# The last feed-forward block's left half by seven products, among the third column block

## The chip, the cores and the metric

The kernel runs on one core of one Trainium2 chip. The metric is the time of one execution on the device in microseconds (us); the time of the kernel before is the median of three runs, 1326.16 us (1325.57 to 1326.43). About 0.2% is what a measurement of this kernel can tell from no change.

## What is computed

One decoder block on 256 tokens of width 2048, all in fp32:

```python
merged = jax.nn.sigmoid(ga) * y_a + jax.nn.sigmoid(gb) * y_b
mix = jnp.einsum('bsd,de->bse', merged, w_out)
h = layer_norm(ALPHA * x + mix, ln1_gain, ln1_bias)
a = jnp.square(jax.nn.relu(jnp.einsum('bsd,df->bsf', h, w_ff1) + b_ff1))
y = layer_norm(ALPHA * h + jnp.einsum('bsf,fd->bsd', a, w_ff2) + b_ff2, ln2_gain, ln2_bias)
```

`w_ff1` is 2048 x 8192 and `w_ff2` 8192 x 2048. `y_a` and `y_b` come from attention and from a gated branch; the change doesn't touch them.

## The kernel before

**Numbers.** Every large product is made of three matmuls in the type fp32r: both operands are split into a high and a low part, and high x high, high x low and low x high are added in PSUM. Activations are split once (`hilo`, L92). Weights are split as they come: a chunk of 512 rows x 512 columns (1 MB) is loaded by SP into one of three `raw` buffers, and used as two pieces of 2 x 128 rows. For each piece ACT writes the high part (L188) and DVE the low part (L157, `emit_low`). When the low part of a chunk's second piece is out, SP's load of the chunk three further on is issued.

**Order.** The program is one list of steps, written by hand; a step is the matmuls of one piece. Each engine works through its own instructions in the order in which they are emitted. `emit_splits` emits splits as far ahead as there are split buffers: the six of RING, so five steps ahead, each taken over when PE has finished the step that used it. Pieces of the last block's column blocks may also use the buffers in LATE. `at(s, f)` emits `f` behind step `s`: that is how evictions' follow-ups, joinings and statistics get their place on DVE.

**Feed-forward.** The 8192 inner columns are worked in eight blocks of 1024. The first layer of a block (steps F) makes `a`; the second layer adds the block's share to `y`, which holds both token tiles (128 tokens each) x 2048. The second layer's columns come in four column blocks of 512. By the plain way (steps E) a column block takes 48 matmuls of 512 columns: 2 token tiles x 8 pieces of 128 rows x 3.

**Seven products.** In the blocks of `SUMMED` (1 to 6 of 0 to 7) column blocks 0 and 1 are made by `products` instead, a Strassen-Winograd scheme: the 2 x 2 arrangement of token tiles and column blocks, and of row halves, takes seven products of 12 matmuls (P1 to P7, 84 in place of 96). It needs sums of activations (`sum_of_acts`, four DVE additions and two splits for each of four pieces) and sums of weights. The sums of weights are made by DMA: POOL loads a block of `w_ff2` into the buffer `held` (L623) and adds other blocks to it with accumulating transfers (L625, L632). There are two such buffers. Buffer 0 holds, one after the other, what P1, P5, P6 and P4 need; the next addition is issued when DVE has written the second low part of the product before:

```python
("P1", plain(0, 0), 0, held_add(u, 0, 1), 0),
("P5", summed(0), 0, held_add(u, 1, 1), 1),
("P6", summed(1), 0, held_add(u, 1, 0), 2),
```

P7 uses buffer 1; P2 and P3 use plain chunks through SP. A product gathers in one of two PSUM buffers named `aux`, in turn, so a product needs the eviction of the last but one. DVE evicts it (L664) into `acc` or `y`. At the end eight joinings (`collect`, L694) add what lies in `acc` to `y`; the sums in `acc` run over all blocks, so these joinings are made once.

**Mixed blocks.** `mixed(b)` interleaves the first layer of block b with the products and steps E of block b - 1, by the list `ORDER` (L36). In it, three steps F stand between P5 and P6.

**The last block and the end.** In the kernel before block 7 takes the plain way: column block 0 for both token tiles, then 1, 2 and 3 for token tile 0, then for token tile 1 (its column block 3 in two halves of 256). The eight joinings lie behind the first steps of it. Statistics (`bn_stats`, 256 columns each) follow each eviction. `ln2_stats` and four `ln2_block`s finish token tile 0 under the matmuls of token tile 1; `ln2_last` (L767) finishes token tile 1 behind the last eviction, with three filling matmuls and one pair of small ones on PE.

**The output projection** is made the same way: P1, P5 and P6 lie among the last groups of the projections before it.

## Time and profile before

| | |
|---|---|
| median of the runs | 1326.16 us |
| profiled execution, its own time | 1326.2 us |
| its span in the profile | 1324.5 us |
| PE busy | 1312.9 us, 99% |
| DVE busy | 939.0 us, 71% |
| ACT busy | 691.0 us, 52% |
| granted TensorE clock, mean | 0.998 |

PE is TensorE, DVE is VectorE, ACT is ScalarE, POOL is GpSimd and SP the engine that issues most loads. Busy time tells which engine is full over the whole span, but matmuls are pipelined and overlap, so a busy PE is not yet PE at its peak. The views by stretch and in order of time tell which wait ends last in one place. In them an instruction has its start, its duration, and in brackets how long its engine stood idle before it and which instruction released it. The 1.7 us between span and time lie outside the profiled program.

### The profile page before, as it was taken

What the parts mean: (1) busy time and instruction counts of PE and PEld (TensorE: products, weight loads), DVE (VectorE), ACT (ScalarE), POOL (GpSimd) and SP (SyncE); (2) the same over time, 40 slices, a digit from 0 to 9 for tenths busy, and PEclk for the clock granted to TensorE, in tenths of its full rate; (3) what the DMA queues carried; (4) which work ended last, traced back from release to release, by engine and by line L of the source; (5) the groups of instructions that cost most, each with busy time, mean ns of one, the idle gap of its engine ahead of it and who ended that gap; (6) DMA issues with size and microseconds to landing.
All of it is one profiled execution on the core that took longest, in us unless ns stands there. A gap on an engine that the chain in (4) does not pass through costs nothing. (4 is left out here: it accounts for less than half of the span.)

```text
span 1324.5 us, 17423 instructions
## 1 busy us (share of the span) xinstructions
PE 1312.9 (99%) x6832; PEld 1111.0 (84%) x6832; DVE 939.0 (71%) x1426; ACT 691.0 (52%) x938; POOL 51.7 (4%) x57
## 2 busy tenths in 40 slices
PE   9999999999999999999999999999999999999998
PEld 6888888888888888889888888888888888888886
DVE  6554678565545689788769768678677796786776
ACT  4444465454544556545545366455555564555641
POOL 0000000000000001000000100010000000100000
PEclk9999999999999999999999999999999999999999
DMA  9866545546555569772874988987887879978561
GB/s 321 289 195 206 176 137 182 191 160 222 191 191 190 187 169 291 244 230 71 283 255 148 284 219 289 248 242 247 217 280 229 237 242 251 252 224 236 178 254 64
DMA packets 140003, 288.83 MB, mean 218 GB/s; under 512 B 5256, under 2 KB 7824, under 8 KB 139024
## 3 DMA queue, kind: packets, MB, share of 16 engines
q1 hardware_dynamic: 120592, 240.26, 53.5%
q0 software_dynamic: 19184, 47.20, 16.8%
q8 instruction: 53, 0.87, 0.3%
q10 hardware_dynamic: 144, 0.26, 0.1%
q14 instruction: 30, 0.25, 0.1%
HBM read 285.59 MB, written 2.11 MB: 217 GB/s over the span
## 5 line engine op out<-in xcount | busy, mean ns | idle before, releaser
L157 DVE TENSOR_TENSOR w<-raw,w 128x1024 fp32r<-128x1024 f32 (+1 forms) x438 | 529.2, 1218 | 300.8 <-ACT w L188 299.7
L188 ACT ACTIVATE w<-raw 128x1024 fp32r<-128x1024 f32 (+1 forms) x438 | 456.7, 1053 | 411.8 <-PE mm L254 289.7
L252 PE MATMUL mm<-hT,w 128*128 128x512 f32 x960 | 339.4, 394 | 0.8 <-DVE sum L277 0.8
L252 PE MATMUL mm<-xs,w 128*128 128x512 f32 x896 | 315.7, 395 | 0.0
L254 PE MATMUL mm<-hT,w 128*128 128x256 f32 x1024 | 276.0, 279 | 0.0
L254 PE MATMUL mm<-xs,w 128*128 128x256 f32 x896 | 250.0, 279 | 0.0
L252 PEld LDWEIGHTS mm<-hT,w 128*128 128x128 f32 x960 | 180.0, 187 | 44.3 <-DVE sum L277 1.1
L252 PEld LDWEIGHTS mm<-xs,w 128*128 128x128 f32 x896 | 167.9, 187 | 39.5
L254 PEld LDWEIGHTS mm<-hT,w 128*128 128x128 f32 x1024 | 188.0, 188 | 2.7
L254 PEld LDWEIGHTS mm<-xs,w 128*128 128x128 f32 x896 | 168.0, 187 | 0.2
L242 PE MATMUL mm<-w,a 128*128 128x512 f32 (+1 forms) x328 | 128.1, 390 | 0.0
L241 PE MATMUL mm<-w,a 128*128 128x512 f32 (+1 forms) x328 | 128.0, 390 | 0.0
L240 PE MATMUL mm<-w,a 128*128 128x512 f32 (+1 forms) x328 | 127.8, 390 | 0.0
L157 DVE TENSOR_TENSOR w<-held,w 128x1024 fp32r<-128x1024 f32 x70 | 85.6, 1223 | 39.3 <-ACT w L188 38.9
L188 ACT ACTIVATE w<-held 128x1024 fp32r<-128x1024 f32 x70 | 73.9, 1058 | 64.7 <-PE mm L242 26.6
L240 PEld LDWEIGHTS mm<-w,a 128*128 128x128 f32 x328 | 61.8, 188 | 14.3
L242 PEld LDWEIGHTS mm<-w,a 128*128 128x128 f32 x328 | 61.7, 188 | 14.0
L241 PEld LDWEIGHTS mm<-w,a 128*128 128x128 f32 x328 | 61.8, 188 | 13.9
L240 PE MATMUL mm<-w,xs 128*128 128x512 f32 x120 | 49.4, 412 | 0.3 <-ACT w L188 0.3
L241 PE MATMUL mm<-w,xs 128*128 128x512 f32 x120 | 47.7, 397 | 1.3 <-DVE w L157 1.3
L277 DVE TENSOR_TENSOR sum<-mm,half 128x256 f32<-128x256 f32 x136 | 48.9, 418 | 0.0
L242 PE MATMUL mm<-w,xs 128*128 128x512 f32 x120 | 47.6, 397 | 0.0
(193 smaller groups left out, 1512.8 us busy)
## 6 DMA issues: line engine op xcount, KB each, us to landing
raw<-in_w_ff_dram SPq DMA_DIRECT2D x116, 1024.0 KB, 6.5
raw<-in_w_in_dram SPq DMA_DIRECT2D x68, 1024.0 KB, 5.1
held<-in_w_ff_dram POOLq DMA_DIRECT2D x36, 1024.0 KB, 8.5
raw<-in_w_out_dram SPq DMA_DIRECT2D x14, 1024.0 KB, 5.4
raw<-in_w_pa_dram SPq DMA_DIRECT2D x8, 1024.0 KB, 5.1
raw<-in_w_pb_dram SPq DMA_DIRECT2D x8, 1024.0 KB, 5.1
held<-in_w_out_dram POOLq DMA_DIRECT2D x6, 1024.0 KB, 8.5
raw<-in_w_in_dram SPq DMA_DIRECT2D x6, 512.0 KB, 7.2
```

The costliest lines, as they stand in the source:

```text
L157: nc.vector.tensor_tensor(h["lo"], sl, f32(h["hi"]), op=ALU.subtract)
L188: nc.scalar.activation(h["hi"], source(h), AF.Copy)
L240: nc.tensor.matmul(p, ah, hi[:, kk, cs], start=first and kk == 0, stop=False)
L241: nc.tensor.matmul(p, ah, lo[:, kk, cs], start=False, stop=False)
L242: nc.tensor.matmul(p, al, hi[:, kk, cs], start=False, stop=last and kk == n - 1)
L252: nc.tensor.matmul(p, hi[:, kk, ws_], av, start=st, stop=False)
L254: nc.tensor.matmul(p[:, :S], lo[:, kk, ws_], av[:, :S], start=False, stop=en)
L277: nc.vector.tensor_tensor(s, p[:, :S], t, op=ALU.add)
```

## The change

Block 7's column blocks 0 and 1 are made by the seven products too (`SUMMED` to 7). Its steps come in a new order, here with h0 and h1 for the two pieces of the second chunk of column block 2:

- column block 2's first chunk (two steps), P1, P3, P2, h0, P5, P7, h1, P6
- column block 3 for token tile 0 (four steps), P4, and column block 3 for token tile 1 in two halves.

The joinings come as soon as their sums are complete: the first behind P1, two behind P5, the others behind P6. Statistics of column blocks 0 and 1 are made by a new function `stats2` behind them. Token tile 0's norm blocks lie behind column block 3's first pass and among P4 and the last halves. The two wide rows of the last norm go to the buffers A4 and A5, since S6 and S13 now hold sums of activations; LATE shrinks to two buffers. In the output projection P5 and P6 come one group later, and the sums of activations are spread over twice as many steps.

```diff
@@ -605,7 +605,7 @@
         return ev
 
     NB = FF // 1024
-    SUMMED = range(1, NB - 1)
+    SUMMED = range(1, NB)
 
 
 
@@ -721,25 +721,30 @@
                     q[:0] = [(h, c == 0 and h == hs[0], c == g.nk // KC - 1 and h == hs[-1]) for h in hs]
             h, f, l = q.pop(0)
             add_step(h, "all", f, l)
-    LATE = ("A4", "A5", "W", "S5", "S10", "S11")
+    LATE = ("W", "S5")
 
     def ev_ff2(blk, c):
         def ev(i, p):
             t, half = i if isinstance(i, tuple) else (i, None)
             y = tiles["y", t][:, c * CW:(c + 1) * CW]
-            if blk == NB - 1 and c == 0:
-                tiles["st2", t] = small.tile([P, 8, 6], F32, name="st2")
+            if blk == NB - 1 and c == 2 and half is None and t == 0:
+                for k in range(NT):
+                    tiles["st2", k] = small.tile([P, 8, 6], F32, name="st2")
             if half is None:
                 nc.vector.tensor_tensor(y, y, p, op=ALU.add)
             else:
                 ys = y[:, half * S:(half + 1) * S]
                 nc.vector.tensor_tensor(ys, ys, p[:, half * S:(half + 1) * S], op=ALU.add)
             if blk == NB - 1:
-                for e in range(2) if half is None else (half,):
-                    nc.vector.bn_stats(tiles["st2", t][:, 2 * c + e, :], y[:, e * S:(e + 1) * S])
+                stats2(t, c, range(2) if half is None else (half,))
                 if c == 3 and half in (None, 1):
                     (ln2_last if t == NT - 1 else ln2_stats)(t)
         return ev
+
+    def stats2(t, c, parts=range(2)):
+        for e in parts:
+            nc.vector.bn_stats(tiles["st2", t][:, 2 * c + e, :],
+                               tiles["y", t][:, c * CW + e * S:c * CW + (e + 1) * S])
 
     def ln2_stats(t):
         mv = small.tile([P, 2], F32, name="mv", bufs=4)
@@ -845,14 +850,14 @@
     for i in range(4):
         add_group(Group(w_pa, i * CW, 8, quad("attnT"), "ws", ev_ya(i)))
         if i >= 2:
-            add_product(("P1", "P6")[i - 2])
+            add_product(("P1", "P5")[i - 2])
         if i == 2:
             for k in range(4):
-                at(len(steps) - 1 + k, lambda k=k: sum_of_acts(("S6", "W"), k, tiles["G", 1][:, 0, k, :]))
+                at(len(steps) - 1 + 2 * k, lambda k=k: sum_of_acts(("S6", "W"), k, tiles["G", 1][:, 0, k, :]))
         add_group(Group(w_pb, i * CW, 8, quad("gmlpT"), "ws", ev_yb(i), after=start_residual if i == 3 else None))
-        if i == 2:
-            at(len(steps), held_load, uo, 1)
-            add_product("P5")
+        if i == 3:
+            at(len(steps) - 3, held_load, uo, 1)
+            add_product("P6")
 
     g = Group(w_out, 2 * CW, 16, quad("merged"), "as", ev_out(2))
     for c, name in enumerate(("P7", "P4", "P3", "P2")):
@@ -913,19 +918,47 @@
                 load_post[j + 2 * i] = [lambda a=a: load_wide(*a)]
         for c in range(4):
             add_group(ff2(b - 1, c))
-    at(len(steps), free.extend, LATE[:4])
-    for i, a in enumerate((("ln2_b", ln2_b, "S6"), ("ln2_g", ln2_g, "S13"))):
+
+
+    at(len(steps), free.extend, LATE)
+    for i, a in enumerate((("ln2_b", ln2_b, "A4"), ("ln2_g", ln2_g, "A5"))):
         load_post[len(chunks) + i] = [lambda a=a: load_wide(*a)]
-    for i in range(8):
-        at(len(steps) + i // 2, collect, ff_unit(0), i)
-    add_group(ff2(NB - 1, 0))
-    hss = [add_pieces(ff2(NB - 1, c)) for c in range(1, 4)]
-    for part, hs in ((0, hss[0]), (0, hss[1]), (0, hss[2]), (1, hss[0]), (1, hss[1]), ((1, 0), hss[2]), ((1, 1), hss[2])):
+    u = ff_unit(NB - 1)
+    prods = products(u)
+    g2, g3 = ff2(NB - 1, 2), ff2(NB - 1, 3)
+
+    def columns2(c):
+        for n, h in enumerate(add_pieces(g2, None, (c,))):
+            add_step(h, "all", c == 0 and n == 0, c == 1 and n == 1)
+
+    def then(*fs):
+        for k, f in enumerate(fs):
+            at(len(steps) + k // 2, *f)
+
+    columns2(0)
+    add_product("P1")
+    then((collect, u, 0))
+    add_product("P3")
+    add_product("P2")
+    hs = add_pieces(g2, None, (1,))
+    add_step(hs[0], "all")
+    add_product("P5")
+    then((collect, u, 1), (collect, u, 6))
+    add_product("P7")
+    add_step(hs[1], "all", False, True)
+    add_product("P6")
+    then(*((collect, u, i) for i in (2, 3)), (stats2, 0, 0), (stats2, 0, 1), *((collect, u, i) for i in (4, 5, 7)),
+         (stats2, 1, 1))
+    hs = add_pieces(g3)
+    for h in hs:
+        s = add_step(h, 0, h == hs[0], h == hs[-1])
+    add_product("P4")
+    then((stats2, 1, 0))
+    for c in range(4):
+        at(s + 1 + c, ln2_block, 0, c)
+    for part in ((1, 0), (1, 1)):
         for h in hs:
-            s = add_step(h, part, h == hs[0], h == hs[-1])
-        if part == 0 and hs is hss[2]:
-            for c in range(4):
-                at(s + 1 + 2 * c, ln2_block, 0, c)
+            add_step(h, part, h == hs[0], h == hs[-1])
 
 
     xr = xT.rearrange("(k p) s -> p k s", p=P)
```

Where instructions stand now, at three places.

DVE's queue, behind the matmuls of the last mixed block. L157 writes a low part (`held` is the buffer of summed weights, `raw` a loaded chunk), L664 evicts a product, L733 or L734 evicts a column block, L694 is a joining. Before:

```order
L664 TENSOR_TENSOR y<-y,aux 128x512
L157 TENSOR_TENSOR w_10710<-raw,w_10710 128x1024
L157 TENSOR_TENSOR w_10725<-raw,w_10725 128x1024
L157 TENSOR_TENSOR w_10742<-raw,w_10742 128x1024
L733 TENSOR_TENSOR y<-y,mm 128x512 x2
L157 TENSOR_TENSOR w_10759<-raw,w_10759 128x1024
L157 TENSOR_TENSOR w_10764<-raw,w_10764 128x1024
```

Now, from P5's first low part to P6's second (P5: w_10845 and w_10855, P7: w_10867 and w_10877, P6: w_10887 and w_10897):

```order
L157 TENSOR_TENSOR w_10845<-held,w_10845 128x1024
L664 TENSOR_TENSOR acc<-acc,aux 128x512
L157 TENSOR_TENSOR w_10855<-held,w_10855 128x1024
L694 TENSOR_TENSOR y<-y,acc 128x512
L157 TENSOR_TENSOR w_10867<-held,w_10867 128x1024
L664 TENSOR_TENSOR y<-y,aux 128x512
L157 TENSOR_TENSOR w_10877<-held,w_10877 128x1024
L157 TENSOR_TENSOR w_10887<-held,w_10887 128x1024
L664 TENSOR_TENSOR y<-y,aux 128x512
L157 TENSOR_TENSOR w_10897<-held,w_10897 128x1024
```

All low parts of the last block read loaded chunks before; now six of these read the buffer of summed weights, and the eviction of P2 (the last L664) stands behind P6's first low part.

POOL's queue at its end, as a difference (L632 is an addition to buffer 0, L623 a plain load, L625 the addition to buffer 1):

```order
 L623 DMA held<-in_w_ff_dram 128x4x512
 L632 DMA held<-in_w_ff_dram 128x4x512 x3
-L1024 UNCONDITIONAL_BRANCH
-L1024 ISA
+L623 DMA held<-in_w_ff_dram 128x4x512
+L625 DMA held<-in_w_ff_dram 128x4x512
+L623 DMA held<-in_w_ff_dram 128x4x512
+L632 DMA held<-in_w_ff_dram 128x4x512 x3
```

Two loads and four additions have come behind what was the end of the queue.

DVE's queue ahead of `ln2_last`, from token tile 0's first norm block (L752 and L760, now L757 and L765) to the last statistics. Before:

```order
L752 SCALAR_TENSOR_TENSOR y<-y,mv,wide 128x512
L760 SCALAR_TENSOR_TENSOR y<-y,ry,wide 128x512
L752 SCALAR_TENSOR_TENSOR y<-y,mv,wide 128x512
L760 SCALAR_TENSOR_TENSOR y<-y,ry,wide 128x512
L733 TENSOR_TENSOR y<-y,mm 128x512
L739 BN_STATS st_10847<-y 128x6 x2
```

Now, with the joining and the statistics that precede it:

```order
L694 TENSOR_TENSOR y<-y,acc 128x512
L746 BN_STATS st_10971<-y 128x6 x2
L757 SCALAR_TENSOR_TENSOR y<-y,mv,wide 128x512
L765 SCALAR_TENSOR_TENSOR y<-y,ry,wide 128x512
L664 TENSOR_TENSOR y<-y,aux 128x512
L757 SCALAR_TENSOR_TENSOR y<-y,mv,wide 128x512
L765 SCALAR_TENSOR_TENSOR y<-y,ry,wide 128x512
L746 BN_STATS st_10971<-y 128x6 x2
```

In place of two column blocks of token tile 1, P4's eviction and the statistics of what it completes now stand among the norm blocks, two more of which follow before the last two evictions.

## Rows read from the trace of the kernel before

**Rows 1.** The page: the span, and busy time of each engine.

```profile
span 1324.5 us, 17423 instructions
...
PE 1312.9 (99%) x6832; PEld 1111.0 (84%) x6832; DVE 939.0 (71%) x1426; ACT 691.0 (52%) x938; POOL 51.7 (4%) x57
```

**Rows 2.** Busy time by stretch: length, then PE, PEld, DVE, ACT, POOL, clock, DMA share, GB/s.

```profile
1260.00:1280.00 20.00, 20.00 (x87) 16.20 (x87) 12.70 (x13) 8.59 (x9) 0.00 (x0) 1.00 1.03 392
1280.00:1313.00 33.00, 33.00 (x168) 27.91 (x167) 27.69 (x54) 3.46 (x4) 0.00 (x0) 1.00 0.10 37
```

**Rows 3.** PE in order of time (start, duration): first and last matmul of block 7.

```profile
1268.50 0.40 PE L240 MATMUL mm<-w,a 128*128 128x512 f32 x1
...
1312.82 0.28 PE L242 MATMUL mm<-w,a 128*128 128x256 f32 x1
```

**Rows 4.** DVE in order of time: the last eviction.

```profile
1313.14 0.42 DVE L736 TENSOR_TENSOR y<-y,mm 128x256 f32<-128x256 f32 x1 [1.95 <-PE mm L242]
```

**Rows 5.** By stretch, `aux` alone: P5 and P6 of the output projection (no POOL column).

```profile
498.97:502.57 3.60, 3.07 (x12) 2.07 (x12) 0.00 (x0) 0.00 (x0) 1.00 1.09 283
513.77:516.57 2.80, 2.80 (x12) 2.08 (x12) 0.00 (x0) 0.00 (x0) 1.00 1.12 198
```

**Rows 6.** Waits of PE from 470 to 1260, longest first: total, times, longest.

```profile
PE mm L252 <- DVE sum L277: 0.8, 1, 0.8
```

**Rows 7.** ACT in order of time: P1's first split in the last two mixed blocks.

```profile
1092.05 1.06 ACT L188 ACTIVATE w<-held 128x1024 fp32r<-128x1024 f32 x1 [1.33 <-PE mm L242]
...
1178.97 1.06 ACT L188 ACTIVATE w<-held 128x1024 fp32r<-128x1024 f32 x1 [1.24 <-PE mm L242]
```

**Rows 8.** DVE in order of time, 1173 to 1180, one block before the end.

```profile
1173.62 3.49 DVE L157 TENSOR_TENSOR w<-raw,w 128x1024 fp32r<-128x1024 f32 x3
1177.03 0.69 DVE L664 TENSOR_TENSOR y<-y,aux 128x512 f32<-128x512 f32 x1
1177.63 2.35 DVE L157 TENSOR_TENSOR w<-raw,w 128x1024 fp32r<-128x1024 f32 x2
```

**Rows 9.** DVE and POOL in order of time: P1's second low part, the addition behind it.

```profile
1182.87 1.22 DVE L157 TENSOR_TENSOR w<-held,w 128x1024 fp32r<-128x1024 f32 x1 [0.39 <-ACT w L188]
1184.47 1.27 POOL L632 DMA_DIRECT2D held<-in_w_ff_dram  x1 [20.67 <-DVE w L157]
```

**Rows 10.** Additions issued at 1010.63, 1184.47, 802.16, 749.05: last column, us to landing.

```profile
held<-in_w_ff_dram POOLq DMA_DIRECT2D x1, 1024.0 KB, 8.4
...
held<-in_w_ff_dram POOLq DMA_DIRECT2D x1, 1024.0 KB, 9.4
...
held<-in_w_ff_dram POOLq DMA_DIRECT2D x1, 1024.0 KB, 13.3
...
held<-in_w_ff_dram POOLq DMA_DIRECT2D x1, 1024.0 KB, 18.0
```

**Rows 11.** DVE in order of time, 1282 to 1305: joinings, an eviction, norm blocks.

```profile
1282.36 0.69 DVE L694 TENSOR_TENSOR acc<-acc 128x512 f32<-128x512 f32 x1
1283.09 0.69 DVE L694 TENSOR_TENSOR y<-y,acc 128x512 f32<-128x512 f32 x1
...
1296.41 0.69 DVE L733 TENSOR_TENSOR y<-y,mm 128x512 f32<-128x512 f32 x1 [1.05 <-PE mm L242]
...
1299.93 0.75 DVE L752 SCALAR_TENSOR_TENSOR y<-y,mv,wide 128x512 f32<-128x512 f32 x1
...
1302.83 0.68 DVE L733 TENSOR_TENSOR y<-y,mm 128x512 f32<-128x512 f32 x1
...
1304.21 0.74 DVE L752 SCALAR_TENSOR_TENSOR y<-y,mv,wide 128x512 f32<-128x512 f32 x1
```

**Rows 12.** By stretch, near the end of the span (the columns of Rows 2).

```profile
1318.00:1319.00 1.00, 0.49 (x1) 0.30 (x2) 0.94 (x2) 0.43 (x2) 0.00 (x0) 1.00 0.00 0
...
1320.00:1321.00 1.00, 0.00 (x0) 0.00 (x0) 0.27 (x1) 0.49 (x1) 0.00 (x0) 0.50 1.03 385
```

**Rows 13.** PE in order of time: the pair of small matmuls in `ln2_last`.

```profile
1318.51 1.35 PE L787 MATMUL aux<-y,dg 128*128 128x512 f32 x2 [1.98 <-ACT dg L783]
```

## The prediction

> **What bounds the kernel now.** I read the page's first part, then the last 55 us. PE is busy for 99% of the span, DVE for 71% [rows 1]. By stretch, PE has no gap from 1260 to 1313, DVE works 40.4 of these 53 us, and the DMA engines are full until 1280 (share 1.03) and nearly idle afterwards (0.10) [rows 2]. The last block's first matmul starts at 1268.50, its last at 1312.82 [rows 3]. DVE keeps up with PE there: for the last eviction it waited 1.95 us [rows 4]. From that eviction, at 1313.14, to the end of the span at 1324.5 are 11.36 us, which I call the ending; the change leaves it as it is. What counts is which engine brings the last eviction, and when.
>
> **The part that should gain.** Columns 0 and 1 of the last block take 96 matmuls now, seven products take 84. Twelve matmuls of 512 columns take PE 2.80 us, 0.233 each [rows 5]: the whole gain on PE there, and the length of a step of 12; one of 6 takes 1.40. Counted from 1268.50, PE without a wait would start P1 at 1274.1, P3 at 1276.9, P2 at 1279.7, h0 at 1282.5, P5 at 1285.3, P7 at 1288.1, h1 at 1290.9, P6 at 1293.7, column 3 of token tile 0 at 1296.5, P4 at 1302.1 and the two last halves at 1304.9 and 1307.7, ending at 1310.5. (h0 and h1 are the two halves of the third column block's second chunk.) In the middle of the program, P5 of the output projection took 3.60 us where P6 took 2.80 [rows 5]; the change gives its sums more time, and the order of POOL's queue there still leaves PE its cover, so I book a gain of 0.8 us, with 0 as the other end.
>
> **The chain of additions.** P5, P6 and P4 read one buffer, to which POOL adds another block of weights after each split. So each waits for: the last split of the product before, the addition, its own split. In the mixed blocks three steps of the first layer, 8.4 us, lie between P5 and P6, too; here only P7 and h1 do, 5.6 us. I follow the chain with durations from rows.
>
> 1. ACT splits the same product in two successive blocks at 1092.05 and 1178.97 [rows 7], so one block is 86.92 us. The block before the last now has the sums of activations, as the one before it had, so I move that one's DVE rows by 86.92. There, three low parts ran 1173.62 to 1177.11, an eviction began at 1177.03 and two more low parts ran 1177.63 to 1179.98 [rows 8]. Those two are now P1's: they end at 1266.9.
> 2. POOL issues 0.38 us after such an end (1182.87 + 1.22 to 1184.47) [rows 9]: at 1267.3.
> 3. Additions landed 8.4 to 9.4 us after their issue in ordinary stretches, and after 13.3 or 18.0 where transfers crowded [rows 10]. The stretch from 1260 to 1280 is crowded now [rows 2]; in the changed program a weight chunk and both rows of the last layer norm are queued there too. I take 11.5, about half way between 9.4 and 13.3: landed at 1278.8. The ends are 8.4 and 18.0.
> 4. ACT's high part takes 1.06 [rows 7], so DVE starts P5's first low part at 1280.0. Low parts follow each other by 1.14 and an eviction costs 0.60 before the next instruction [rows 8]: P5's second low part ends at 1280.0 + 1.14 + 0.60 + 1.22 = 1282.96. The addition for P6 is issued at 1283.3 and, in quieter DMA, lands 8.5 later at 1291.8; P6's first low part starts on DVE at 1293.05.
> 5. DVE had come to that instruction at 1286.5 (a joining 0.65, two low parts, an eviction). It waits 6.5 us with everything else behind it, P2's eviction included, which stands behind it in DVE's queue. P7 needs P2's PSUM buffer, since the products share two: it starts at 1293.05 + 1.14 + 0.68 = 1294.9 instead of 1288.1. **PE stands for 6.8 us.**
> 6. P6's second low part ends at 1296.0, the addition for P4 goes out at 1296.4 and lands at 1304.9; P4's first low part starts at 1306.05. DVE has only 7.2 us of other work in between and loses another 3 us.
>
> **DVE from there.** P4's two low parts, 2.3; two evictions with their statistics, 1.38 each (1302.83 to 1304.21) [rows 11], 2.76. Then P6's eviction and two dependent joinings, 0.73 each until the last (1282.36 to 1283.09) [rows 11], 2.06; four statistics, 1.34; two joinings, 1.33; the eviction of column 3, its statistics and the reciprocal root, 3.52 (1296.41 to 1299.93); a joining and statistics, 1.39; four norm blocks of 1.45 (two between 1299.93 and 1302.83), 5.8 [rows 11]; P4's eviction and statistics, 1.27. That is 2.3 + 2.76 + 16.7 = 21.8: DVE reaches the first of the two last evictions at 1327.8, some 15 us after PE has finished it, and the last one 0.85 later, at 1328.7. With the ending of 11.36 the span is 1340.0.
>
> Two corrections. PE idles for over 10 us before the last small matmuls. After it had stood from 1316.5, but for 1.35 us of work, its granted clock read 0.50 at 1320, the 1.2 GHz level, against 1.00, the 2.4 GHz level, at 1318 [rows 12]. Those two matmuls took 1.35 us [rows 13]; at half the clock they would cost up to 1.35 more; I take 0.7. The output projection gives 0.8 back. Span 1339.9. The profiled execution took 1326.2 for a span of 1324.5, so 1.7 us lie around it, and its time equals the median of the three runs (1326.16). **Forecast: 1341.6 us**, slower by 1.2%.
>
> **Edits at no cost.** The wide rows go to other buffers, free long before; fewer weight chunks are loaded. ACT has 3.46 us of work in the last 33 [rows 2], so its extra splits are covered until it too waits for the additions. The sums of activations in the block before are covered by PE there, as in the blocks before: from 470 to 1260 PE's longest wait is 0.8 us [rows 6].
>
> **Ends of the forecast itself.** All three additions in 8.4 us and no clock loss: 1338.7 - 0.8 + 1.7 = 1339.6. First addition 13.3, the other two 9.4, full clock loss, nothing from the output projection: 1341.6 + 1.8 + 1.8 + 0.65 + 0.8 = 1346.7. An 18.0 alone would add 6.5.
>
> The row that decides most is the landing under crowding [rows 10]: with 8.4 for the first addition alone the sum is 1340.5, since other low parts keep DVE until 1278.9 anyway, with 13.3 it is 1343.4. The Trainium skill (DMA: Bandwidth & Descriptors, section on queues, rings and completion order) says that each DMA engine takes turns, packet by packet, between the queues that have work for it, which speaks against this change: POOL's addition shares with SP's loads. By that rule the sum would be the 1343.4, and by the ordinary rows the 1340.5.
>
> **Rivals.**
> - *DVE alone, transfers in time* (8%). DVE's work from 1268.65 to the first of the last evictions, by the prices above: two evictions, 1.2; 17 low parts, 19.4; five evictions, 3.0; three joinings, 1.95; 2.76 and 16.7 as above. Together 45.0, against 39 us of PE. P2's splits get their buffers only as PE leaves them, which costs 3.3 us. So the last eviction starts at 1317.8, the span is 1329.2 less the 0.8 and plus the 0.7, the time 1330.8. For it: in the mixed blocks splits of the held buffer wait for PE, not for a transfer [rows 7]. It needs P6's addition down by 1286.5, about 4 us after its issue; against it stands every row of an addition.
> - *PE stays the bound, faster* (4%). Place: the last eviction. Price: the 2.80 us come through, span 1324.5 - 2.8 - 0.8 = 1320.9, time 1322.6. It decides where DVE reaches the first half of column 3 by 1307.7. For it: the same seven products cost PE next to no wait in the mixed blocks [rows 6]. Against it: 45.0 us of work in 39.
> - *The array stays slow after the stall* (5%). After 6.8 us of standing PE goes on at the 1.2 GHz level and doesn't recover: the 22.4 us of matmuls from 1294.9 take 44.8 and end at 1339.7, the span is 1351 and the time 1352. For it: the fall at 1320 [rows 12]. Against it: PE would be working again without a gap. The Trainium skill (TensorE: Matmul & The Clock Gate, part on the HAM clock gate) says that the gate opens again under sustained work. By that, a few steps run at half speed inside PE's spare 10 us, and the sum stays; no run here shows it.
> - The change does what it says by the order of its instructions, so I give nothing to its not acting. 3% are left for mixtures that end within 0.2%.
>
> **Numbers.** About 0.2%, 2.7 us, is what a measurement of this kernel can tell from no change. The forecast has 80%. The range goes from the DVE rival to the slow end of the forecast, 1330 to 1347; outside lie the fast rival, the slow array and a first addition of 18. Faster 4%, same 3%, slower 93%.
>
> **What would show it.** In the changed profile: P7's first matmul waits for DVE's eviction by some 7 us; ACT's splits of the held buffer wait for its transfer twice, about 9 and 7 us; DVE's low parts wait for ACT by about 6.5 and 3 us; the last two evictions on DVE have no wait for PE before them and start some 10 us after PE's last matmul. The forecast is wrong if PE shows no gap before P7, if additions land in under 5 us, or if DVE's last evictions wait for PE again.

## The result and the profile after

The changed kernel takes **1357.23 us** (median of four runs, 1355.80 to 1358.15); the kernel before, run beside it, 1325.98 us (1325.57 to 1326.43). The ratio is 1.0235, with an interval from 1.0217 to 1.0252. The forecast was 1341.6 us with a range from 1330 to 1347: slower, as predicted, but by 31 us where 15.6 were forecast. The time lies outside the range.

The page of the changed kernel: span, and busy time of each engine. It answers to [rows 1].

```profile
span 1355.5 us, 17474 instructions
...
PE 1317.1 (97%) x6820; PEld 1111.3 (82%) x6820; DVE 952.5 (70%) x1459; ACT 698.8 (52%) x952; POOL 58.3 (4%) x63
```

PE has twelve matmuls less to do. Its busy time is longer all the same; matmuls behind a stop run at a lower clock, as the stretches below show. The span is 31.0 us longer than before. Two places hold nearly all of it.

**The first place is in the middle of the program, some 740 us ahead of the last block.** The changed kernel in order of time (start, duration, engine, and in brackets the idle time and its releaser), around P7 of the output projection:

```profile
519.54 1.25 POOL L632 DMA_DIRECT2D held<-in_w_out_dram  x1 [14.87 <-DVE w L157]
520.29 1.29 POOL L623 DMA_DIRECT2D held<-in_w_out_dram  x1
533.21 1.27 POOL L625 DMA_DIRECT2D held<-in_w_out_dram  x1 [11.62 <-DMA raw<-in_w_out_dram]
...
541.77 1.06 ACT L188 ACTIVATE w<-held 128x1024 fp32r<-128x1024 f32 x1 [21.49 <-DMA held<-in_w_out_dram]
...
542.88 0.79 PE L212 MATMUL aux<-w,ca 128*128 128x512 f32 x1 [9.61 <-ACT w L188]
```

The first row is the addition for P4, which POOL issues only when DVE has written P6's second low part. P6 now comes one group later. Behind that addition, in the same queue, stands the load of buffer 1 (L623), and behind that the addition to buffer 1 (L625), which waits until the load has landed. The load took 12.6 us, beside P4's addition and a weight chunk, and the addition behind it 8.5 us; they end at about 541.7. In the kernel before, load and addition of buffer 1 went out ahead of P4's addition (L632):

```profile
501.00 0.78 POOL L623 DMA_DIRECT2D held<-in_w_out_dram  x1 [6.47 <-DVE cb L578]
508.07 1.26 POOL L625 DMA_DIRECT2D held<-in_w_out_dram  x1 [6.29 <-DMA held<-in_w_out_dram]
510.02 1.27 POOL L632 DMA_DIRECT2D held<-in_w_out_dram  x1 [0.69 <-DVE w L157]
```

P7 reads buffer 1: in the changed kernel ACT waits 21.49 us for it, and PE stands 9.61 us, where before it had no wait over 0.8 us in all of this stretch [rows 6].

The same place by stretch: length, then PE, PEld, DVE, ACT, POOL, granted clock, DMA share, GB/s.

```profile
540.00:545.00 5.00, 1.66 (x3) 1.05 (x4) 2.15 (x5) 2.37 (x6) 0.00 (x0) 0.50 1.05 391
545.00:550.00 5.00, 4.91 (x15) 3.22 (x15) 4.47 (x9) 3.63 (x5) 0.00 (x0) 0.69 0.16 67
550.00:560.00 10.00, 10.00 (x45) 8.03 (x44) 9.73 (x15) 8.01 (x11) 0.00 (x0) 1.00 0.37 109
```

After it had stood, PE went on at a granted clock of 0.50, the 1.2 GHz level, and was back at 1.00 by 550. P7's twelve matmuls took from 542.88 to 548.86, 5.98 us in place of 2.80 (0.5 of it a wait for a low part). So this place costs 9.6 + 3.2 = 12.8 us.

**The second place is the last block**, as forecast. In order of time, the three additions, ACT's first split behind each, and DVE's first low part behind that split; this answers to [rows 9] and [rows 10]:

```profile
1280.30 1.29 POOL L632 DMA_DIRECT2D held<-in_w_ff_dram  x1 [16.71 <-DVE w L157]
1294.74 3.90 ACT L188 ACTIVATE w<-held 128x1024 fp32r<-128x1024 f32 x4 [4.60 <-DMA held<-in_w_ff_dram]
1295.83 1.23 DVE L157 TENSOR_TENSOR w<-held,w 128x1024 fp32r<-128x1024 f32 x1 [4.05 <-ACT w L188]
...
1299.10 1.26 POOL L632 DMA_DIRECT2D held<-in_w_ff_dram  x1 [17.51 <-DVE w L157]
1307.48 2.00 ACT L188 ACTIVATE w<-held 128x1024 fp32r<-128x1024 f32 x2 [8.84 <-DMA held<-in_w_ff_dram]
1308.57 1.23 DVE L157 TENSOR_TENSOR w<-held,w 128x1024 fp32r<-128x1024 f32 x1 [6.31 <-ACT w L188]
...
1311.90 1.27 POOL L632 DMA_DIRECT2D held<-in_w_ff_dram  x1 [11.54 <-DVE w L157]
1320.50 2.01 ACT L188 ACTIVATE w<-held 128x1024 fp32r<-128x1024 f32 x2 [7.21 <-DMA held<-in_w_ff_dram]
1321.59 1.23 DVE L157 TENSOR_TENSOR w<-held,w 128x1024 fp32r<-128x1024 f32 x1 [3.12 <-ACT w L188]
```

The additions landed 14.3, 8.3 and 8.5 us after their issue. Each time ACT, and behind it DVE, stands until the transfer is down; DVE loses 4.05 + 6.31 + 3.12 = 13.5 us in three waits. PE in order of time, the first matmuls of P2 and of P7:

```profile
1297.80 0.77 PE L212 MATMUL aux<-w,a 128*128 128x512 f32 x1 [5.03 <-ACT w L188]
...
1310.54 0.48 PE L212 MATMUL aux<-w,ca 128*128 128x512 f32 x1 [2.06 <-ACT w L188]
```

The rows name ACT, but its splits for P2 had been written by 1290.1. What ended last is DVE's eviction of P1, which stands behind P5's first low part in DVE's queue, and for P7 the eviction of P2, which stands behind P6's. The two evictions:

```profile
1296.97 0.68 DVE L664 TENSOR_TENSOR acc<-acc,aux 128x512 f32<-128x512 f32 x1
...
1309.72 0.68 DVE L664 TENSOR_TENSOR y<-y,aux 128x512 f32<-128x512 f32 x1
```

This is how a transfer that DVE waits for stops PE as well.

DVE and PE in order of time at the end, which answers to [rows 4] and [rows 13]:

```profile
1343.25 0.41 DVE L737 TENSOR_TENSOR y<-y,mm 128x256 f32<-128x256 f32 x1
...
1344.04 0.41 DVE L737 TENSOR_TENSOR y<-y,mm 128x256 f32<-128x256 f32 x1
...
1333.57 0.28 PE L242 MATMUL mm<-w,a 128*128 128x256 f32 x1
...
1349.40 2.07 PE L792 MATMUL aux<-y,dg 128*128 128x512 f32 x2 [12.12 <-ACT dg L788]
```

The two last evictions have no wait for PE any more. PE had ended its last matmul of the second layer (L242) at 1333.85, 9.4 us before the first of them. DVE sets the end.

### The profile page after: what moved, and what is told of

Read it like the earlier page. It is cut to its first block, busy times and chain, and to the rows that moved or that the text cites. A ratio compares the mean times of both kernels' runs of the same rounds, so it can differ in the third digit from the quotient of the medians.

```text
span 1355.5 us, 17474 instructions
## 1 busy us (share of the span) xinstructions
PE 1317.1 (97%) x6820; PEld 1111.3 (82%) x6820; DVE 952.5 (70%) x1459; ACT 698.8 (52%) x952; POOL 58.3 (4%) x63
## 4 chain that ended last, share of the span: by engine, by line
PE 83%; DVE 7%; DMA 6%; ACT 1%; issue 1%; SPq 0%; ACTq 0%; DVEq 0%; POOLq 0%
PE mm L252 33%; PE mm L254 17%; PE mm L241 7%; PE mm L242 7%; PE mm L240 7%; DMA held<-in_w_ff_dram 4%; DVE w L157 3%; PE aux L213 3%; PE aux L214 3%; PE aux L212 3%; ACT w L188 1%; DMA raw<-in_w_out_dram 1%; PE mm L257 1%; DMA held<-in_w_out_dram 1%; DMA raw<-in_w_in_dram 1%
## 5 line engine op out<-in xcount | busy, mean ns | idle before, releaser
L157 DVE TENSOR_TENSOR w<-raw,w 128x1024 fp32r<-128x1024 f32 (+1 forms) x434 | 523.6, 1218 | 289.7 <-ACT w L188 288.7
L157 DVE TENSOR_TENSOR w<-held,w 128x1024 fp32r<-128x1024 f32 x80 | 97.6, 1222 | 72.3 <-ACT w L188 72.0
L188 ACT ACTIVATE w<-held 128x1024 fp32r<-128x1024 f32 x80 | 83.9, 1056 | 104.7 <-DMA held<-in_w_ff_dram 34.4
L242 PE MATMUL mm<-w,a 128*128 128x512 f32 (+1 forms) x296 | 115.5, 390 | 0.0
L241 PE MATMUL mm<-w,a 128*128 128x512 f32 (+1 forms) x296 | 115.4, 390 | 0.0
L240 PE MATMUL mm<-w,a 128*128 128x512 f32 (+1 forms) x296 | 115.3, 389 | 0.0
L240 PEld LDWEIGHTS mm<-w,a 128*128 128x128 f32 x296 | 55.8, 188 | 12.9
L242 PEld LDWEIGHTS mm<-w,a 128*128 128x128 f32 x296 | 55.7, 188 | 12.7
L241 PEld LDWEIGHTS mm<-w,a 128*128 128x128 f32 x296 | 55.8, 188 | 12.5
L212 PE MATMUL aux<-w,ca 128*128 128x512 f32 x128 | 51.5, 402 | 11.7 <-ACT w L188 11.7
L213 PE MATMUL aux<-w,ca 128*128 128x512 f32 x128 | 51.7, 404 | 1.0 <-DVE w L157 0.9
L214 PE MATMUL aux<-w,ca 128*128 128x512 f32 x128 | 51.2, 400 | 0.0
L240 PE MATMUL mm<-w,xs 128*128 128x512 f32 x120 | 49.5, 412 | 0.2 <-ACT w L188 0.2
```

The costliest lines, as they stand in the source:

```text
L157: nc.vector.tensor_tensor(h["lo"], sl, f32(h["hi"]), op=ALU.subtract)
L188: nc.scalar.activation(h["hi"], source(h), AF.Copy)
L212: nc.tensor.matmul(p, ah, hi[:, kk], start=first and kk == 0, stop=False)
L213: nc.tensor.matmul(p, ah, lo[:, kk], start=False, stop=False)
L214: nc.tensor.matmul(p, al, hi[:, kk], start=False, stop=last and kk == n - 1)
L240: nc.tensor.matmul(p, ah, hi[:, kk, cs], start=first and kk == 0, stop=False)
```

## The experiments

Times are medians. Unless another base is named, "before" is the kernel before in the runs of the same group, 1325.97 to 1326.37 us; so differences between kernels of different groups are good to about 0.4 us. The rows are those of one execution of each kernel.

**1 to 3. Where the unforeseen 15 us lie.** Three kernels: the changed kernel with the old order of the output projection; the kernel before with only the new one; and the changed kernel with buffer 1's load two steps earlier.

```diff
 # out_as_before: after, with before's lines at this place
-            add_product(("P1", "P5")[i - 2])
+            add_product(("P1", "P6")[i - 2])
...
-        if i == 3:
-            at(len(steps) - 3, held_load, uo, 1)
-            add_product("P6")
+        if i == 2:
+            at(len(steps), held_load, uo, 1)
+            add_product("P5")
 # out_alone: before, with after's lines at this place
 # load_early: after, with
-            at(len(steps) - 3, held_load, uo, 1)
+            at(len(steps) - 5, held_load, uo, 1)
```

out_as_before, expected:

> The changed kernel with the output projection's order as it was before (the last block stays changed). Theory, two places: the projection's buffer 1 is loaded behind P6's addition on POOL and costs some 13 us there, the last block some 17 to 18 us. Then this kernel takes 1357.2 - 12.9 = about 1344 us, and PE's wait of 9.6 us before P7 of the projection is gone. Rival, last block alone: what PE loses in the projection is given back later, and this kernel stays at 1357 us.

Measured: 1343.15 us (1342.92 to 1343.30), ratio 1.0128 [1.0113, 1.0144]. That is 14.1 us less than the changed kernel; PE's wait before P7 of the projection is gone.

out_alone, expected:

> The kernel before with only the new order in the output projection. Theory, two places: 1326.0 + 12.9 = about 1339 us, with PE's wait of 9 to 10 us for the projection's P7 and half the clock behind it. Rival, last block alone: 1326 us, no change.

Measured: 1337.52 us (1337.18 to 1337.98), ratio 1.0086 [1.0071, 1.0101]: 11.2 us slower than before, with the last block untouched. PE waits 8.8 us for P7 there.

load_early, expected:

> The changed kernel with one number changed: the load of the projection's buffer 1 is issued two steps earlier, so that it stands before P6's addition in POOL's queue. Theory, POOL's queue: the wait before P7 of the projection goes, POOL starts that load some 15 us earlier (near 505 in place of 520), and the time is 1343.5 to 1344.3 us. Rival, the products' new places or the spread sums cost it: PE still waits there and the time stays above 1350 us.

Measured: 1342.13 us (1341.79 to 1342.63), ratio 1.0121 [1.0106, 1.0136]: 15.1 us less than the changed kernel, with one number changed. PE has no wait left between 450 and 620. POOL in order of time shows why:

```profile
507.37 0.78 POOL L623 DMA_DIRECT2D held<-in_w_out_dram  x1 [3.38 <-DVE cb L578]
516.20 1.26 POOL L625 DMA_DIRECT2D held<-in_w_out_dram  x1 [8.05 <-DMA held<-in_w_out_dram]
518.86 1.27 POOL L632 DMA_DIRECT2D held<-in_w_out_dram  x1 [1.41 <-DVE w L157]
```

Load and addition of buffer 1 now stand ahead of P4's addition, which waits for DVE. The load goes out at 507.37 instead of 520.29. All kernels below but the next are built on load_early.

**4. Is the rest of the new order worth something by itself?** load_early_alone is the kernel before with load_early's lines in the projection.

> The kernel before with nothing but the output projection's new order, buffer 1's load two steps earlier as in load_early. Theory: P5 of the projection then stands for nothing (3.60 us before, 2.80 after) and the last block is untouched, so about 0.8 to 1.0 us faster than before, some 1325.4. Rival: the stall of 0.8 us at P5 was only moved to another step of the projection: 1326.2 to 1326.4, no change.

Measured: 1325.84 us (11 runs, 1324.99 to 1327.03), ratio 0.9996 [0.9987, 1.0005]. The stall inside P5 [rows 5] is gone from the trace (its twelve matmuls start within 2.56 us, 3.26 before), but a gain of 0.8 us in the time can neither be shown nor excluded: 0.3 was measured, and the interval goes from 1.7 us faster to 0.7 slower. In the traces PE is 0.78 us shorter over this stretch: from P1's first matmul to P2's last it takes 75.96 us (484.99 to 560.95) in place of 76.74 (484.87 to 561.61), and load_early and out_as_before differ there by the same. Behind it, up to 1245, PE waits 1.1 us for the splits of products where before it waited 0.5, so most of the gain is lost again in this execution.

**5. Does DVE's wait for the additions make the rest?** In no_additions the additions in block 7 are left out, so P5, P6 and P4 use P1's block. In load_early the three low parts behind an addition are these (DVE, in order of time):

```profile
1280.87 1.22 DVE L157 TENSOR_TENSOR w<-held,w 128x1024 fp32r<-128x1024 f32 x1 [2.96 <-ACT w L188]
...
1293.41 1.22 DVE L157 TENSOR_TENSOR w<-held,w 128x1024 fp32r<-128x1024 f32 x1 [6.11 <-ACT w L188]
...
1306.19 1.23 DVE L157 TENSOR_TENSOR w<-held,w 128x1024 fp32r<-128x1024 f32 x1 [2.88 <-ACT w L188]
```

```diff
     u = ff_unit(NB - 1)
+    held_add = lambda u, r, c: None
     prods = products(u)
```

> load_early without block 7's three additions of weights: P5, P6 and P4 use the block that P1 uses, so the sums of weights are left out of the computation; the number of matmuls, splits, evictions and joinings stays. Theory (DVE waits for the additions, then works without a gap): the three waits of 2.96, 6.11 and 2.88 us go, 1342.1 - 12.0 = 1330.2, and DVE's last evictions still come without a wait for PE, about the 1330.8 of the rival DVE alone in the prediction. Rival, PE would be the bound without them: 1322.6. Rival, the waits are not what costs: 1340 to 1342.

Measured: **1330.48 us** (1329.94 to 1331.51), ratio 1.0030 [1.0018, 1.0042]. The three waits were 11.95 us in load_early, and 11.65 us went with them. PE's waits for P2 and P7 shrank with them to one of 0.9. DVE in order of time, the first of the two last evictions:

```profile
1317.54 0.41 DVE L737 TENSOR_TENSOR y<-y,mm 128x256 f32<-128x256 f32 x1
```

It has no wait for PE even here, and DVE has no wait for anything between 1278 and this row, so DVE's own work is longer than PE's. (The trace is of the execution that took 1331.51 us.)

**6. How far is DVE above PE?** no_adds_no_joins also leaves out the eight calls of `collect`.

> no_additions with the eight joinings left out as well, so the products' sums in acc are never added to y; DVE has eight instructions of 0.65 us, 5.2 us, less. Theory (DVE is the bound even without the additions): 1330.2 - 5.2 = 1325.0. Rival, PE is the bound already without the additions, or the joinings lie in waits: no change from no_additions.

Measured: 1327.57 us (10 runs, 1326.73 to 1330.00), ratio 1.0010 [1.0001, 1.0019]. Only 2.9 of the 5.2 us came through. DVE in order of time, the eviction of column block 3 of token tile 0:

```profile
1305.43 0.69 DVE L734 TENSOR_TENSOR y<-y,mm 128x512 f32<-128x512 f32 x1 [1.97 <-PE mm L242]
```

DVE now waits for PE there, 1.97 us, which with 0.40 us of smaller waits for ACT is about what is missing of the 5.2: the two engines are level, and the end behind this eviction (its statistics, the root, four norm blocks) is DVE's again. The trace is of the longest of the ten executions, 1330.00 us; it is later than load_early's by 3.1 us already ahead of the last block (the same low part, P3's second, starts at 1271.84 and 1268.79), so the lateness doesn't bear on this wait.

**7 and 8. What crowds the first addition?** The wide rows of the last norm, 1 MB each, go out from SP at 1263.48 and 1270.46 in load_early. wide_late moves them two chunks later, wide_early some 20 us earlier.

```diff
 # wide_late
-        load_post[len(chunks) + i] = [lambda a=a: load_wide(*a)]
+        load_post[len(chunks) + 2 + i] = [lambda a=a: load_wide(*a)]
 # wide_early
-        load_post[len(chunks) + i] = [lambda a=a: load_wide(*a)]
+        at(len(steps) - 12 + 2 * i, load_wide, *a)
```

wide_late, expected:

> As load_early, and the two wide rows of the last norm are loaded two weight chunks later, so that they don't share the DMA engines with the first addition of the last block (14 us from issue to landing in the changed kernel). Theory, crowding: that addition lands in 8.5 to 10 us, DVE's wait of 4 us for it goes, and the kernel is 3 to 4.5 us faster than load_early, about 1340 us. Rival, DVE's own work or the later additions set the end anyway: less than 1 us faster than load_early.

Measured: 1341.39 us (1340.29 to 1342.17), ratio 1.0115 [1.0098, 1.0132], 0.7 less than load_early, and the runs of the two overlap. DVE in order of time, P5's and P6's first low parts:

```profile
1277.30 1.22 DVE L157 TENSOR_TENSOR w<-held,w 128x1024 fp32r<-128x1024 f32 x1
...
1292.60 1.23 DVE L157 TENSOR_TENSOR w<-held,w 128x1024 fp32r<-128x1024 f32 x1 [8.89 <-ACT w L188]
```

The wait before P5's low part is gone: the first addition landed in 8.5 us. But the wide rows now went out at 1275.55 and 1276.10, and the second addition, issued at 1280.56, took 10.9 us. Its wait grew from 6.11 to 8.89 us. The crowding had moved to the next addition.

wide_early, expected:

> load_early with the two wide rows loaded some 20 us earlier, behind the last first-layer step of block 7 (about 1242 us), where the DMA engines had room (share 0.67 from 1240 to 1260 in load_early); no transfer is added. Theory (the chain has two parts, the crowding by the wide rows and the chain itself): the first addition lands 8.4 us after its issue at 1266.4, DVE has no wait before P5's low parts, so P6's addition is issued at 1280.6, lands 8.5 later, and P6's low part starts at 1290.3 where it started at 1293.4; waits of about 3.0 us are left there and 2.9 before P4's: 1342.1 - 3.1 = 1339.0, of which 8.5 us above no_additions are the chain itself. Rival, the crowding moves to a transfer before (P1's block or a chunk, between 1245 and 1270): 1341 to 1344. Rival, additions take 13 us anyway: 1342.

Measured: **1339.29 us** (1339.10 to 1339.34), ratio 1.0100 [1.0083, 1.0117], 2.8 less than load_early. DVE in order of time, the same two low parts and P4's:

```profile
1278.25 1.22 DVE L157 TENSOR_TENSOR w<-held,w 128x1024 fp32r<-128x1024 f32 x1
...
1290.77 1.23 DVE L157 TENSOR_TENSOR w<-held,w 128x1024 fp32r<-128x1024 f32 x1 [6.09 <-ACT w L188]
...
1303.64 1.23 DVE L157 TENSOR_TENSOR w<-held,w 128x1024 fp32r<-128x1024 f32 x1 [2.97 <-ACT w L188]
```

The three additions landed in 8.5, 8.1 and 8.3 us, about the shortest of this case, and the waits of 6.09 and 2.97 stay: they are the chain itself, split to addition to split.

**9 and 10. Can the chain be broken?** two_buffers gives P6 and P4 a third buffer, filled from 1233 on; P5's low parts then issue no addition, and the wide rows go to two other buffers. two_buffers_late also loads the wide rows two chunks later.

```diff
+    def third_load(u):
+        tiles["b", 2] = big.tile([P, KC, CW], F32, name="third", tag="A4")
+        nc.gpsimd.dma_start(tiles["b", 2], block(u, 0, 0))
...
-    prods = products(u)
+    prods = products(u, two=2)
+    n = len(steps)
+    at(n - 13, third_load, u)
+    at(n - 8, held_add(u, 0, 1, 2))
+    at(n - 4, held_add(u, 1, 1, 2))
```

two_buffers, expected:

> load_early with a third buffer: the sum for P6 is made in a buffer of its own from about 1240 us on, while PE works on block 6, and P4's addition follows P6's splits there; the buffer of P1 gets the addition for P5 only; the wide rows go to two other free buffers. Nothing is left out, 2 MB more are moved. Theory (each product waits for an addition that waits for the splits of the product before): the waits of 6.11 and 2.88 us on DVE go, that of 2.96 us before P5 stays: 1342.1 - 9.0 = 1333.1. Rival, the 2 MB more crowd the chunk loads between 1240 and 1270 and PE waits there: 1336 to 1342. Rival, DVE's waits are not what costs: 1342.

Measured: 1342.55 us (1341.86 to 1343.41), ratio 1.0122 [1.0106, 1.0137]: no gain. DVE's waits for the additions for P6 and P4 shrank from 6.11 and 2.88 us to none and 1.46, but the first addition now took 18.9 us, and DVE waited 3.31 us for a chunk and 5.10 for that addition. This is the crowding of the first rival, though DVE met it and not PE, and somewhat later, from 1278 on.

two_buffers_late, expected:

> two_buffers with the two wide rows loaded two chunks later, as in wide_late. In two_buffers the first addition landed 19 us after its issue, DVE waited 3.31 us for a chunk and 5.10 for that addition, and 2.9 elsewhere. Theory (every transfer that is waited for is late only because the wide rows and the third buffer's blocks crowd the same 20 us): the addition issued at 1266.8 lands by about 1277 to 1279, the 8.4 us shrink to 0 to 2, and nothing behind it waits for an addition: 1342.5 minus 6.5 to 9.5, so 1333 to 1336, at the best the 1330.5 of no_additions. Rival, the wait moves on again as in wide_late, to a chunk or to P4's addition: 1339 or more.

Measured: 1341.21 us (1340.46 to 1341.35), ratio 1.0112 [1.0094, 1.0130]: the rival again. By stretch, two_buffers_late:

```profile
1240.00:1260.00 20.00, 20.00 (x88) 16.11 (x87) 19.20 (x45) 14.00 (x23) 2.12 (x2) 1.00 0.99 307
1260.00:1280.00 20.00, 20.00 (x86) 15.82 (x84) 13.39 (x15) 7.85 (x9) 2.55 (x2) 1.00 1.06 277
```

ACT of the same kernel in order of time:

```profile
1278.68 2.01 ACT L188 ACTIVATE w<-raw 128x1024 fp32r<-128x1024 f32 x2 [3.12 <-DMA raw<-in_w_ff_dram]
1285.04 3.90 ACT L188 ACTIVATE w<-held 128x1024 fp32r<-128x1024 f32 x4 [4.36 <-DMA held<-in_w_ff_dram]
```

In load_early the DMA share from 1240 to 1260 was 0.67; with 2 MB more it is 0.99, and 1.06 after it. P6's low parts no longer wait for an addition, but a chunk comes 3.12 us late and P5's addition took 17.5 us. The waits went from the chain to the transfers: DVE's add up to 9.7 us behind 1277, where load_early had the 11.95. The third buffer with the wide rows loaded early, as in wide_early, was not run.

**11 and 12. Less work on DVE.** joins_on_pool is two_buffers_late with the eight joinings on GpSimd; norms_on_pool moves two norm blocks to ACT and GpSimd as well.

```diff
-            nc.vector.tensor_tensor(d, a, b, op=op)
+            (nc.gpsimd if u.key == "ff" else nc.vector).tensor_tensor(d, a, b, op=op)
 # norms_on_pool, norm blocks 0 and 1 of token tile 0
...
+        nc.scalar.activation(z, z, AF.Identity, bias=tiles["neg2"], scale=tiles["r2", t])
+        nc.gpsimd.tensor_tensor(z, z, tiles["ln2_g"][:, sl], op=ALU.mult)
+        nc.gpsimd.tensor_tensor(z, z, tiles["ln2_b"][:, sl], op=ALU.add)
```

joins_on_pool, expected:

> two_buffers_late with the last block's eight joinings on GpSimd in place of DVE. Theory (DVE bounds the end; no_adds_no_joins gained 2.9 us where DVE lost 5.2 us of work, since DVE then waited 2 us for PE): 2.5 to 3.5 us faster than two_buffers_late. Rival, GpSimd takes so long for a joining, or for the chain of four that need each other, that DVE's statistics wait for them: same as two_buffers_late or slower.

Measured: 1339.92 us (1338.69 to 1340.51), ratio 1.0105 [1.0087, 1.0123]. 1.3 us less than two_buffers_late, about half of what was expected; the runs of the two kernels overlap. The rival came true in part: GpSimd's chain of joinings kept DVE's statistics waiting for 2.16 us.

norms_on_pool, expected:

> joins_on_pool with two of the four norm blocks of token tile 0 made by one ACT instruction and two GpSimd ones each, in place of two DVE ones each. Theory (DVE is still the bound): 2 * 1.45 = 2.9 us less on DVE between the last statistics of token tile 0 and the last two evictions, of which the wait for PE takes some: 1 to 2.9 us faster than joins_on_pool, at the best about 1324. Rival, the end waits for PE or for GpSimd's last block: no change or slower.

Measured: 1341.62 us (1340.91 to 1341.75), ratio 1.0115 [1.0099, 1.0131]: 1.7 us more than joins_on_pool: the rival's outcome, but not its mechanism, since the last two evictions wait for neither PE nor GpSimd there. The last section shows what the rows give for both. No version that was run beats the kernel before by more than a measurement can tell.

## Why the prediction was half right

**The 31 us, step by step.** Each difference is between two medians above, and the four add up from 1326.2 to 1357.2:

| from | to | us | what it is |
|---|---|---|---|
| after 1357.23 | load_early 1342.13 | 15.1 | buffer 1's load behind P4's addition, in the output projection; see below |
| load_early | wide_early 1339.29 | 2.8 | wide rows beside the first addition |
| wide_early | no_additions 1330.48 | 8.8 | the chain of additions |
| no_additions | before 1326.16 | 4.3 | DVE's own work, longer than PE's, net of PE's 2.80 |

Of the 15.1 us the rows show 13.0 between P1 and P2 of the projection, 12.8 of them the stop and the slow matmuls behind it. Another 1.0 is the first addition of the last block, which landed in 14.3 and 13.3 us. And 0.7 was there ahead of the place (P1 of the projection starts at 485.26 and 484.58), which the one changed number doesn't touch. no_additions has the wide rows where load_early has them, so the split between the second and the third row of the table holds for this order of steps. In out_alone the same stop was 8.8 us and the matmuls behind it 2.75 longer, about 11.5 us together, beside the 11.2 measured.

**The step that failed** is the sentence "the change gives its sums more time, and the order of POOL's queue there still leaves PE its cover, so I book a gain of 0.8 us, with 0 as the other end". The order of POOL's queue says the opposite. In the kernel before, load and addition of buffer 1 stand ahead of the third L632, in the changed one behind it (left before, right now, in the output projection):

```
L632 DMA held<-in_w_out_dram 128x4x512 x2     L632 DMA held<-in_w_out_dram 128x4x512 x3
L623 DMA held<-in_w_out_dram 128x4x512        L623 DMA held<-in_w_out_dram 128x4x512
L625 DMA held<-in_w_out_dram 128x4x512        L625 DMA held<-in_w_out_dram 128x4x512
L632 DMA held<-in_w_out_dram 128x4x512
```

I had followed a moved step's matmuls and sums but not the queue that its load was moved past. The prices were at hand: P7 needs two transfers in series, a load and an addition. An addition takes 8.4 to 18.0 us by [rows 10], the load took 7 in the kernel before, and a pair that starts behind P6's low parts has only the steps from there to P7 as cover. The pair took until 541.7, and P7 was due at 533.1. That the bound was closed at zero made it worse: the other end of this term was not 0 but a stall, and the range had no room for it. Experiments 1 to 3 show the cause from both sides.

**The term that was mis-sized** is the first addition, taken as 11.5 us: it landed in 14.3, and in 13.3 in load_early, so DVE's wait before P5's first low part was 4.05 and 2.96 us and not 1.1. Of the two rows between which the prediction halved, 9.4 and 13.3, the higher was the nearer one. Of the rival prices by the rule on queues (the Trainium skill, DMA: Bandwidth & Descriptors, section on queues, rings and completion order: an engine takes turns, packet by packet, between queues that have work), the slower fits. The traces agree in so far as a transfer lands later beside others: 8.5 us without the wide rows, 13.3 with them, and 17.5 in two_buffers_late, where another addition ran beside it until 1276.9 and the wide rows from 1277.3 on. Turns by packets no row shows. The prediction's 1343.4 for 13.3 us stands beside 1342.13 for load_early.

**What held.** P1's second low part was forecast to end at 1266.9, and POOL's addition to go out at 1267.3; in load_early, without the stall, it went out at 1266.42, about 0.8 of the difference being the shorter stretch of the projection (experiment 4). P6's first low part was to wait 6.5 us, and waited 6.31; P4's 3, and waited 3.12. PE was to stand 6.8 us before P7; it stood 5.03 before P2 and 2.06 before P7, 7.1 together. The place was off because the prediction followed P2's eviction but not P1's, which stands behind P5's first low part. By its own numbers (1280.0 + 1.14 + 0.68) that eviction ended at 1281.8, and P2 was due at 1279.7. Even with the additions left out PE waits 0.9 us for it. From P6's first low part to the first of the last evictions 34.75 us were added up from [rows 8] and [rows 11]; 34.68 were measured. The whole: 13.0 us from the projection at the first addition's issue, net of what the new order gained there, the 0.8 booked for it besides, 2.5 more up to P6's first low part, and 0.7 less behind it make the 15.6 by which the forecast was short. One sum in the prediction is off: DVE was to reach the first of the two last evictions some 15 us after PE, and by its own numbers (1327.8 less 1307.7 and 6.8) it is 13.3. Nothing else hangs on it.

**The last matmuls** took 2.07 us where they took 1.35, the 0.7 of the text. But the span's end moved hardly at all by it: from the last eviction to the end 11.46 us in place of 11.36, so this term should have been near 0.

**The rivals.** *DVE alone, transfers in time* was priced at 1330.8; with the additions away 1330.48 was measured. The mechanism is right (P2's splits held DVE up for 3.17 us, 3.3 were priced), and its condition is what the kernel lacks. That the price agrees to 0.3 us owes something to luck: the 0.8 taken off and the 0.7 put on, neither of which is borne out by the time, nearly cancel. *PE stays the bound* needed DVE's work to be shorter than PE's; it isn't: with 5.2 us of work taken off DVE besides the additions (experiment 6) the time is still 5 us above this rival's 1322.6. *The array stays slow after the stall* fell, in both places. After the 9.6 us in the projection the clock read 0.50, then 0.69, then 1.00, once PE worked without a gap. In the last block, behind the waits before P2 and P7:

```profile
1300.00:1310.00 10.00, 8.49 (x32) 6.49 (x30) 3.69 (x5) 2.52 (x3) 0.36 (x1) 0.88 0.61 105
1310.00:1315.00 5.00, 4.46 (x19) 3.68 (x20) 5.00 (x6) 3.29 (x4) 1.27 (x1) 1.00 0.20 18
```

That agrees with the Trainium skill (TensorE: Matmul & The Clock Gate, part on the HAM clock gate), by which the gate opens again under sustained work. It isn't free, though: P7 of the projection took 3.2 us longer.

**What stays open.** Whether the 0.8 us that the projection's new order gains on PE reach the end of the program (experiment 4). Whether a block 7 by seven products can beat the kernel before was not settled: it would need sums of weights that are made without crowding the last 40 us, and less DVE work than any version here has.

## What to carry to other kernels

When a load is moved, read the queue it is issued from, not only the steps it serves: in POOL's queue here everything behind an instruction that waited for DVE waited too, and the two transfers in series behind it (12.6 and 8.5 us) had to fit into the work that was left before their product. When a chain runs split, transfer, split on one buffer, count its links against the work that lies between them; fewer matmuls are worth nothing if the chain sets the pace. And before a transfer is moved out of the way of another, look at the DMA share of the place it goes to, and at what else is waited for there: the two wide rows gained 2.8 us in a stretch whose share rose from 0.67 to 0.90 by them; beside the next addition they only moved the wait, and so did the third buffer's blocks, which filled the same stretch to 0.99 and ran on beside the addition.

## What the runs showed of the hardware

**A GpSimd operation stretches DVE's beside it where DVE reads two inputs from SBUF.** joins_on_pool, POOL and DVE in order of time:

```profile
1285.72 2.19 POOL L698 TENSOR_TENSOR y<-y,acc 128x512 f32<-128x512 f32 x1 [18.92 <-DVE acc L668]
1285.56 3.44 DVE L157 TENSOR_TENSOR w<-held,w 128x1024 fp32r<-128x1024 f32 x2
...
1298.83 4.44 POOL L698 TENSOR_TENSOR y<-y,acc 128x512 f32<-128x512 f32 x2 [3.65 <-DVE acc L668]
1298.66 3.45 DVE L157 TENSOR_TENSOR w<-raw,w 128x1024 fp32r<-128x1024 f32 x2
1302.03 0.67 DVE L668 TENSOR_TENSOR acc<-acc,aux 128x512 f32<-128x512 f32 x1
...
1312.07 0.75 DVE L750 BATCH_NORM_STATS2 st<-y 128x6 f32<-128x256 f32 x2 [2.16 <-POOL y L698]
```

norms_on_pool, a norm block on POOL and one on DVE at the same time:

```profile
1320.71 1.28 POOL L784 TENSOR_TENSOR y<-y,wide 128x512 f32<-128x512 f32 x1 [2.76 <-ACT y L783]
1322.07 1.59 POOL L785 TENSOR_TENSOR y<-y,wide 128x512 f32<-128x512 f32 x1
...
1321.08 1.46 DVE L761 SCALAR_TENSOR_TENSOR y<-y,mv,wide 128x512 f32<-128x512 f32 x1
1322.57 1.64 DVE L769 SCALAR_TENSOR_TENSOR y<-y,ry,wide 128x512 f32<-128x512 f32 x1
```

Two low parts take 2.35 us elsewhere [rows 8], and 3.44 and 3.45 beside a joining on GpSimd; a norm instruction takes 0.75 alone [rows 11], and 1.46 to 1.64 here. The eviction at 1302.03 reads one of its inputs from PSUM, and beside the same GpSimd operations it took its usual 0.67. A joining on GpSimd took 2.2 us beside the low parts and about 1.3 in joins_on_pool after 1309, where none stood beside it, against 0.69 on DVE.

In experiment 11 the eight joinings took 5.2 us off DVE. The two stretched pairs gave back 2.2 of them, and the wait of 2.16 for GpSimd's joining at 1312.07 as much again. In experiment 12 the four norm instructions left on DVE beside GpSimd's took 6.5 us in place of 3.0: 3.5 more, against the 2.9 taken off. About 1 us of its loss is another thing: the first addition took 18.1 us there and 17.1 in joins_on_pool.

The Trainium skill (SBUF — State Buffer, section on the two separate sides) says that the two engines share a pair of ports under an exclusive lock when DVE reads two inputs from SBUF and GpSimd reads too; the rows shown agree, since only such operations of DVE took longer in them.

**A stop of 9.6 us costs PE a third more than its length**, since the 12 matmuls behind it ran mostly at the lower clock: 12.8 us in all, the 0.5 for a low part included.
